# The head of a decoder layer: filler products between conditioning bursts, and an order for the first tokens written out

## The chip, the core and the metric

The kernel runs on one core of one Trainium2 chip. A core has a matrix engine (TensorE, PE in the profile; its weight loads are shown as PEld), a vector engine (VectorE, DVE), a scalar engine (ScalarE, ACT), a general engine (GpSimd, POOL) and a queue engine that issues transfers (SyncE, SP). Transfers run on 16 DMA engines that all queues share. The metric is the device time of one execution in microseconds. Before the change it was 1991.17 us, the median of three runs between 1989.67 and 1992.51.

## The reference, cut to what matters

```python
mod = jax.nn.silu(c) @ w_ada + b_ada                       # c: one row for the prompt, 8 for the samples
sh1, sc1, g1, sh2, sc2, g2 = [m[:, None, :] for m in jnp.split(mod, 6, axis=-1)]
h = _rmsnorm(x, norm1_g) * (1 + sc1) + sh1                 # x: 256 prompt tokens and 64 sample tokens, 2048 wide
p = h @ w_in                                               # 11,280 columns: q, k, v, og, u, ga, gb, alr
...                                                        # linear attention, pooling, gates, feed-forward
```

All of it is float32. This case is about the first lines only: the conditioning product `silu(c) @ w_ada` for the shift and scale of the first norm (sections 0 and 1 of six), the normed tokens `h`, and the first products of `h` with `w_in`.

## The kernel before, in words

**Layout.** The 320 tokens are kept transposed: a tile has 128 of the 2048 model columns on its partitions and the 320 tokens (T; TP = 256 prompt, TS = 64 sample) along its row, so there are 16 token tiles, KT = 16. A weight matrix is read in blocks of rows; each block lands in a buffer named raw, is copied by ScalarE to a rounded high part (whi, line 152), and VectorE takes the difference as the low part (wlo, line 153). Every product of weights with tokens is then three TensorE products (lines 166 to 168): high weights by high tokens (hh), high weights by low tokens (hl), low weights by high tokens, each 128 x 128 by 320 columns. There are three raw buffers in the main weight pool and five buffers each of whi and wlo.

**The head.** The conditioning rows c are loaded, transposed by 16 small TensorE transposes, and passed through a sigmoid to give scT. The tokens come in three tiles xn of 128, 128 and 64 rows, 2048 wide, all by SyncE's queue ahead of the first conditioning weights. A loop over the 16 token tiles makes three TensorE transposes each into a bank of `misc()` (four PSUM banks in rotation) and copies the bank to xT, on ScalarE and VectorE in turn (line 462). The sums of squares, the reciprocal root, and its broadcast rx follow (lines 473 to 486). `HeadJob` then makes the conditioning for some token tiles: `load` (line 414) issues two blocks of w_ada of 512 KB, `burst` (line 422) issues loads ahead and 32 small products in four column strips of the array (line 218), and `finish` (line 434) copies, transposes and adds the bias, so that the shift and scale (mod) stand ready. The job of the first two token tiles has four bursts over eight blocks; its blocks have eight buffers (araw). `h_unit` (line 488) then makes hh and hl of a token tile on VectorE, GpSimd and ScalarE.

**Stages.** The projection by w_in goes over five slices of token tiles, SLICES = (0,2), (2,4), (4,8), (8,12), (12,16). For each slice, a loop takes 15 units of 256 weight columns in the order q, k, v, v, u, og, og, ga, ga, gb, gb and four more gb; units of v and of the gates go by two from one block of 512 columns (`proj_pair`, line 197). After each unit, `after_unit` runs a share of a background list that prepares the next slice: the spill of xT to DRAM by GpSimd's queue, the next HeadJob's load, its four bursts and its finish, and the h_units. So in the first slice the first load comes after the second v, and the first burst (with four more loads) after u.

**What sets the order.** A scheduler orders the instructions of each engine by a simulated timeline, except those that pass through `tc.keep_in_program_order`, here also called `pinned`, which keep the order of the program among themselves. In the head all weight loads on SyncE's queue are of that kind (line 144 follows the flag in_order), and the queue is served in order: a load whose buffer is still in use holds back those behind it. For the first slice this order is, before the change: the 8 blocks of w_ada for the first job; the blocks of q, k and v; two blocks of w_ada for the second job; the block of u; four blocks of w_ada; the block of og; two blocks of w_ada; the blocks of ga and of the gbs.

Of the kernel before, what the change touches and what calls it, by code (L numbers as in the profile page):

```python
# [20 lines left out]
P = 128  # L21
TP, NB, LS = 256, 8, 8
TS = NB * LS
T = TP + TS
D = 2048
KT = D // P
# [10 lines left out]
WB = 5  # L37
AB = 3
SLICES = ((0, 2), (2, 4), (4, 8), (8, 12), (12, 16))
# [41 lines left out]
def body(tc, A):  # L81
    nc = tc.nc
    ctx = ExitStack()
    cp = ctx.enter_context(tc.tile_pool(name="cp", bufs=1))
    wp = ctx.enter_context(tc.tile_pool(name="wp", bufs=3))
# [41 lines left out]
    def tr(out, in_):  # L127
        k = in_.shape[0]
        PE.transpose(out, in_, ident[:k, :k])  # L129
# [5 lines left out]
    def raw_chunk(src, nk, nn, pool=None, tag="raw", bufs=3):  # L135

        if pool is None and more:
            more.reverse()
            if more[0] is not None:
                pool, bufs = more[0], 2  # L140
        t = (pool or wp).tile([P, nk, nn], F32, tag=tag, bufs=bufs, name=nm("raw"))
        ins = nc.sync.dma_start(t, src)
        if in_order[0]:
            tc.keep_in_program_order(ins)
        return t
# [7 lines left out]
        V.tensor_sub(lo, raw, hi.bitcast(F32))  # L153
# [16 lines left out]
    def proj(w, col, k0, k1, xh, xl):  # L170

        ps = pmain.tile([P, 2, 512], F32, tag="pm", name=nm("ps"))
        for c0 in range(k0, k1, 4):
            nk = min(4, k1 - c0)
            for j, whi, wlo in split_chunk(w[:, c0:c0 + nk, col:col + 256], nk, 256):
# [20 lines left out]

    def proj_pair(w, col, k0, k1, xh, xl):

        parts = list(split_chunk(w[:, k0:k1, col:col + 512], k1 - k0, 512))
# [171 lines left out]
    def units(h):  # L371
        return [("q", 0, OQ + DK * h), ("k", 0, OK_ + DK * h), ("v", 0, OV + DV * h),
                ("v", 1, OV + DV * h + 256), ("u", 0, OU + 256 * h),
                ("og", 0, OOG + DV * h), ("og", 1, OOG + DV * h + 256),
                ("ga", 0, OGA + DV * h), ("ga", 1, OGA + DV * h + 256),
                ("gb", 0, OGB + DV * h), ("gb", 1, OGB + DV * h + 256)]


    with tc.tile_pool(name="head", bufs=1) as xp:
# [17 lines left out]
        nc.gpsimd.dma_start(vr1[64:68, :], A["gla_norm_g"][0].rearrange("(r p) -> r p", p=P))  # L397
        pt = misc()
# [4 lines left out]
        S.activation(csig, crT, AF.Sigmoid)  # L403
        V.tensor_tensor(scT[:, :, 0:9], crT, csig, op=ALU.mult)

        def pinned(ins):
            tc.keep_in_program_order(ins)

        class HeadJob:


            def __init__(self, b0, s):
                self.b0, self.s, self.w, self.nk = b0, s, 64 * s, 8 // s
                self.ps = None
                self.raws = {}
# [19 lines left out]
            def finish(self):  # L435
                nb = self.s // 2
                sb = xp.tile([P, 2 * P], F32, tag="adasb", name=nm("adasb"))
                S.copy(sb[:, 0:self.w], self.ps[:, 0:self.w])
# [11 lines left out]


        xT = []
        for k in range(KT):
            pt = misc()
            for i in range(3):
                n = P if i < 2 else TS
                tr(pt[:, i * P:i * P + n], xn[i][:n, k * P:(k + 1) * P])
            if k < SLICES[0][1]:
                xT.append(xp.tile([P, T], F32, name="xT%d" % k))
            else:  # L460
                xT.append(hp.tile([P, T], F32, tag="hl%d" % k, name="xT%d" % k))
            (S.copy if k % 2 else V.tensor_copy)(xT[k], pt[:, 0:T])

        pt = misc()
        tr(pt[:, 0:96], vr0)
        tr(pt[:, 96:164], vr1)
# [5 lines left out]
        ssq = xp.tile([P, 3], F32, name="ssq")  # L472
        V.memset(ssq, 1.0)
        for i in range(3):
            n = P if i < 2 else TS
            S.activation(junk[:n], xn[i][:n], AF.Square, accum_out=ssq[:n, i:i + 1])
        S.activation(ssq, ssq, AF.Sqrt, scale=1.0 / D, bias=epst)
        V.reciprocal(ssq, ssq)
        prs = misc()
        dg = xp.tile([P, 3, P], F32, name="dg")  # L480
        for i in range(3):
            n = P if i < 2 else TS
            V.tensor_scalar(dg[:n, i, :n], ident[:n, :n], ssq[:n, i:i + 1], None, op0=ALU.mult)
            PE.matmul(prs[:, i * P:i * P + n], lhsT=ones[:n, :], rhs=dg[:n, i, :n], start=True, stop=True)
        rx = xp.tile([P, T], F32, name="rx")
        V.tensor_copy(rx, prs[:, 0:T])

        def h_unit(k):
            t = xp.tile([P, T], F32, tag="xh", bufs=2, name=nm("xh"))
            V.scalar_tensor_tensor(t[:, 0:TP], xT[k][:, 0:TP], modp(1, k), rx[:, 0:TP], op0=ALU.mult, op1=ALU.mult)  # L490
            G.tensor_tensor(t[:, TP:T], xT[k][:, TP:T], rx[:, TP:T], op=ALU.mult)
            G.tensor_tensor(s3(t[:, TP:T]), s3(t[:, TP:T]), mods(1, k), op=ALU.mult)
            G.tensor_tensor(s3(t[:, TP:T]), s3(t[:, TP:T]), mods(0, k), op=ALU.add)
            S.activation(hh[k][:, 0:TP], t[:, 0:TP], AF.Identity, bias=modp(0, k))
            S.copy(hh[k][:, TP:T], t[:, TP:T])
            hl[k] = hp.tile([P, T], F32R, tag="hl%d" % k, name="hl%d" % k)
            V.scalar_tensor_tensor(hl[k][:, 0:TP], t[:, 0:TP], modp(0, k), hh[k][:, 0:TP].bitcast(F32),
                                   op0=ALU.add, op1=ALU.subtract)
            V.tensor_sub(hl[k][:, TP:T], t[:, TP:T], hh[k][:, TP:T].bitcast(F32))  # L499
# [682 lines left out]
```

## Time and profile before

| | |
|---|---|
| median of three runs | 1991.17 us |
| the profiled execution | 1994.81 us, of which 1993.0 us from the first to the last instruction |
| mean granted TensorE clock | 0.991 |
| first burst of conditioning products starts | 27.1 us |
| last burst of the first job ends | 33.3 us |
| first product with w_in starts | 36.66 us |

Times inside the profile are counted from the first instruction of the profiled execution. In the rows, a line number is that of the code printed above, out<-in are the program's tile names, and xN is a count of merged instructions. The view of stretches gives each engine's busy time, the granted TensorE clock, the share of the DMA engines' time, and the rate.

### The profile page before, as it was taken

To read this page: it belongs to the slowest core of one execution; us is meant where nothing else is said; L and a number is where in the kernel's file an instruction comes from. 1 tells how busy PE (TensorE), PEld (TensorE's weight loads), DVE (VectorE), ACT (ScalarE), POOL (GpSimd) and SP (SyncE) were. 2 spreads that over 40 slices of the span, in tenths; PEclk is the share of its full clock that TensorE was granted. 3 is DMA by queue.
4 is the path that set the end of the run, shared out by engine and by line. 5 is a ranking of instruction groups with operands and counts; after the bars stand their busy time and mean duration, and the time that the engine had idled before them with its cause. 6 is when DMAs were issued, how large, how long until landed. Compare 5 with 4: busy or idle time off the path is not lost.

```text
span 1993.0 us, 37189 instructions
## 1 busy us (share of the span) xinstructions
PE 1944.7 (98%) x15014; PEld 1850.7 (93%) x15014; DVE 1014.1 (51%) x1883; ACT 819.7 (41%) x1467; POOL 138.0 (7%) x261
## 2 busy tenths in 40 slices
PE   7999999999999999999989999999999999999997
PEld 5789998898999899889989999999999999999997
DVE  2556665474546544664474444444444444444554
ACT  4333364353336433653354333343333334344443
POOL 1112220111010100110030000000000000000000
PEclk9999999999999999999989999999999999999998
DMA  8888754775975787579637666544444444444443
GB/s 290 289 298 264 231 174 144 264 267 183 326 247 162 277 274 232 169 256 323 227 113 226 202 213 200 161 155 145 150 147 153 150 152 152 150 148 147 148 138 97
DMA packets 322558, 400.83 MB, mean 201 GB/s; under 512 B 13545, under 2 KB 262633, under 8 KB 322049
## 3 DMA queue, kind: packets, MB, share of 16 engines
q1 hardware_dynamic: 310114, 358.21, 55.9%
q0 software_dynamic: 12272, 40.25, 5.4%
q8 instruction: 117, 1.92, 0.4%
q14 instruction: 55, 0.45, 0.1%
HBM read 373.96 MB, written 24.67 MB: 200 GB/s over the span
## 4 chain that ended last, share of the span: by engine, by line
PE 93%; DMA 3%; DVE 1%; ACT 1%; issue 1%; SPq 0%; POOL 0%; DVEq 0%; ACTq 0%; POOLq 0%
PE ps L166 27%; PE ps L168 27%; PE ps L167 27%; PE pm L218 5%; PE pm L129 2%; DMA raw<-w_ada 2%; PE pm L804 1%; PE pm L825 1%; DMA raw<-w_in 1%; PE pm L773 1%; DMA xn<-x_prompt 1%; DMA x<-xspill 0%; PE pm L800 0%; PE pm L762 0%; DVE wlo L153 0%
## 5 line engine op out<-in xcount | busy, mean ns | idle before, releaser
L153 DVE TENSOR_TENSOR wlo<-raw,whi 128x512 fp32r<-128x512 f32 x953 | 658.0, 695 | 819.6 <-ACT whi L152 815.1
L152 ACT CAST whi<-raw 128x512 fp32r<-128x512 f32 x953 | 586.4, 621 | 997.2 <-PE ps L167 832.4
L166 PE MATMUL ps<-hh,whi 128*128 128x320 f32 x1408 | 443.2, 315 | 6.7 <-ACT whi L152 3.3
L166 PE MATMUL ps<-h2h,whi 128*128 128x320 f32 x1408 | 437.7, 311 | 5.1 <-ACT h2h L1046 5.1
L168 PE MATMUL ps<-hh,wlo 128*128 128x320 f32 x1408 | 440.8, 313 | 0.2 <-DVE wlo L153 0.2
L167 PE MATMUL ps<-hl,whi 128*128 128x320 f32 x1408 | 438.8, 312 | 0.4 <-DVE hl L499 0.4
L168 PE MATMUL ps<-h2h,wlo 128*128 128x320 f32 x1408 | 435.7, 310 | 0.0
L167 PE MATMUL ps<-h2l,whi 128*128 128x320 f32 x1408 | 435.7, 310 | 0.0
L166 PEld LDWEIGHTS ps<-hh,whi 128*128 128x128 f32 x1408 | 265.5, 189 | 25.6 <-issue 10.2
L168 PEld LDWEIGHTS ps<-hh,wlo 128*128 128x128 f32 x1408 | 265.7, 189 | 8.6 <-issue 5.7
L166 PEld LDWEIGHTS ps<-h2h,whi 128*128 128x128 f32 x1408 | 265.2, 188 | 8.2 <-ACT h2h L1046 5.8
L167 PEld LDWEIGHTS ps<-hl,whi 128*128 128x128 f32 x1408 | 265.8, 189 | 7.5 <-issue 5.9
L167 PEld LDWEIGHTS ps<-h2l,whi 128*128 128x128 f32 x1408 | 265.2, 188 | 0.0
L168 PEld LDWEIGHTS ps<-h2h,wlo 128*128 128x128 f32 x1408 | 265.0, 188 | 0.0
L166 PE MATMUL ps<-ah,whi 128*128 128x320 f32 x704 | 218.5, 310 | 0.0
L168 PE MATMUL ps<-ah,wlo 128*128 128x320 f32 x704 | 217.7, 309 | 0.0
L167 PE MATMUL ps<-al,whi 128*128 128x320 f32 x704 | 217.6, 309 | 0.0
L167 PEld LDWEIGHTS ps<-al,whi 128*128 128x128 f32 x704 | 132.2, 188 | 0.0
L166 PEld LDWEIGHTS ps<-ah,whi 128*128 128x128 f32 x704 | 132.2, 188 | 0.0
L168 PEld LDWEIGHTS ps<-ah,wlo 128*128 128x128 f32 x704 | 132.2, 188 | 0.0
L218 PE MATMUL pm<-raw,scT 128*32 128x128 f32 (+1 forms) x2688 | 105.1, 297 | 5.9 <-DMA raw<-w_ada 5.9
L218 PEld LDWEIGHTS pm<-raw,scT 128*32 128x32 f32 x2688 | 72.3, 112 | 26.9 <-issue 13.8
(289 smaller groups left out, 1541.5 us busy)
## 6 DMA issues: line engine op xcount, KB each, us to landing
raw<-w_ada SPq DMA_DIRECT2D x192, 512.0 KB, 6.2
raw<-w_gu SPq DMA_DIRECT2D x176, 512.0 KB, 3.5
raw<-w_in SPq DMA_DIRECT2D x173, 512.0 KB, 4.4
raw<-w_down SPq DMA_DIRECT2D x79, 512.0 KB, 3.3
S<-state_gla POOLq DMA_DIRECT2D x16, 1024.0 KB, 8.3
o_gs<-S POOLq DMA_DIRECT2D x16, 1024.0 KB, 7.4
raw<-w_o SPq DMA_DIRECT2D x32, 512.0 KB, 5.0
raw<-w_down SPq DMA_DIRECT2D x15, 256.0 KB, 2.5
```

Source lines behind the costliest of these rows:

```text
L129: PE.transpose(out, in_, ident[:k, :k])
L152: S.copy(hi, raw)
L153: V.tensor_sub(lo, raw, hi.bitcast(F32))
L166: PE.matmul(ps, lhsT=whi, rhs=xhi, start=start, stop=False)
L167: PE.matmul(ps, lhsT=whi, rhs=xlo, start=False, stop=False)
L168: PE.matmul(ps, lhsT=wlo, rhs=xhi, start=False, stop=stop)
L218: ins = PE.matmul(ps[32 * j:32 * j + 32, 0:w], lhsT=scT[:, k, :], rhs=raws[j], start=k == 0 if start is None else start, stop=k == KT - 1 ...
L773: PE.matmul(pt, lhsT=E["kdn"][:, s, d * P:(d + 1) * P], rhs=E["vn"][:, s], start=s == 0, stop=s == 1)
L804: PE.matmul(pt[32 * j:32 * j + 32, :], lhsT=qeP[:, d, 4 * gg + j, :], rhs=E["S0", gg, d][:, j], start=False, stop=d == 1, tile_position=(0 ...
L825: PE.matmul(pt, lhsT=kpz[:, gg, j, d * P:(d + 1) * P], rhs=E["vp"][:, gg], start=True, stop=True)
```

## The change: what it does

The change rewrites the head, up to the first slice's loop; the loop itself and all after it are unchanged.

- **Filler.** A tile fill of 128 x 512 ones is made, and `keep_busy(n)` puts n products of 512 columns into a PSUM tile that nobody reads. There are 6 before the transposes of c, 3 after them, 10, 7 and 3 after the transposes from the three x tiles, and 4 after each of the first three bursts. All of them, the transposes of c and x, and the first strip of each conditioning product are kept in program order on TensorE.
- **Transposes.** Only the first three token tiles are transposed before the first burst; tiles 3 to 6, 7 to 11 and 12 to 15 follow the first, second and third burst. The norm's broadcast comes ahead of the third burst.
- **x_sample.** Its transfer is issued by ScalarE's queue behind the sigmoid, no longer by SyncE's queue behind x_prompt.
- **First tokens.** rx times xT is made ahead for tiles 0 and 1 (xhat), and `h_first` makes hh and hl of these tiles with all its steps in program order; tile 0's sample part goes to VectorE instead of GpSimd.
- **First weights.** The blocks of q, k, v and u are issued right after the last burst in the program; their high and low parts (`EarlySplit`) stand in program order on ScalarE and VectorE: the copy of `finish`, high of q, the steps of token tile 0, low of q, high of k, the steps of tile 1, low of k, then the rest. On SyncE's queue the block of u now stands ahead of the second job's first two blocks of w_ada.

```diff
-    def split_chunk(src, nk, nn):
+    ready = {}
+    class EarlySplit:
+        def __init__(self, raw):
...
+            self.h = wp.tile([P, 512 // n, n], F32R, tag="whi", bufs=WB, name=nm("whi"))
+            self.l = wp.tile([P, 512 // n, n], F32R, tag="wlo", bufs=WB, name=nm("wlo"))
+        def hi(self):
+            tc.keep_in_program_order(S.copy(self.h, self.raw))
+        def lo(self):
+            tc.keep_in_program_order(V.tensor_sub(self.l, self.raw, self.h.bitcast(F32)))
...
-        nc.sync.dma_start(xn[2][0:TS], A["x_sample"].rearrange("b t d -> (b t) d"))
+        idle = pmain.tile([P, 2, 512], F32, tag="pm", name=nm("idle"))
+        fill = xp.tile([P, 512], F32R, name="fill")
...
+        def keep_busy(n, tiled=0):
+            for _ in range(n):
+                tc.keep_in_program_order(PE.matmul(idle[:, 0, :], lhsT=fill[:, 0:P], rhs=fill, start=True, stop=True))
...
+        keep_busy(6)
         pt = misc()
         for k in range(KT):
-            tr(pt[:, 16 * k:16 * k + 9], crow[:, k * P:(k + 1) * P])
+            ptr(pt[:, 16 * k:16 * k + 9], crow[:, k * P:(k + 1) * P])
+        keep_busy(3)
...
+        tc.keep_in_program_order(S.activation(csig, crT, AF.Sigmoid))
+        tc.keep_in_program_order(nc.scalar.dma_start(xn[2][0:TS], A["x_sample"].rearrange("b t d -> (b t) d")))
...
+        pts = [misc() for _ in range(NX0)]
+        for i in range(3):
+            n = P if i < 2 else TS
+            for k in range(NX0):
+                ptr(pts[k][:, i * P:i * P + n], xn[i][:n, k * P:(k + 1) * P])
+            keep_busy((10, 7, 3)[i])
...
+        def h_first(k):
+            t = xhat[k]
+            E = G if k else V
+            pinned(S.activation(hh[k][:, 0:TP], t[:, 0:TP], AF.Identity, scale=modp(1, k), bias=modp(0, k)))
+            pinned(E.tensor_tensor(s3(t[:, TP:T]), s3(t[:, TP:T]), mods(1, k), op=ALU.mult))
+            pinned(E.tensor_tensor(s3(t[:, TP:T]), s3(t[:, TP:T]), mods(0, k), op=ALU.add))
+            pinned(S.copy(hh[k][:, TP:T], t[:, TP:T]))
+            hl[k] = hp.tile([P, T], F32R, tag="hl%d" % k, name="hl%d" % k)
+            pinned(V.tensor_scalar(t[:, 0:TP], t[:, 0:TP], modp(1, k), modp(0, k), op0=ALU.mult, op1=ALU.add))
+            pinned(V.tensor_sub(hl[k], t, hh[k].bitcast(F32)))
...
-        for f in HeadJob(0, SLICES[0][1]).steps():
-            f()
-        for k in range(SLICES[0][1]):
-            h_unit(k)
+        for i, k0 in enumerate(range(0, KT, 4)):
+            if i == 2:
+                x_norm()
+            job0.burst(k0)
+            while len(xT) < (7, 12, 16, 16)[i]:
+                x_trans(len(xT), len(xT) % 2)
+            if i < 3:
+                keep_busy(4)
+        ew = []
+        for kind, i, col in units(0)[:5]:
...
+            raw = raw_chunk(win[:, 0:nx, col:col + (512 if kind == "v" else 256)], nx, 512 if kind == "v" else 256)
...
+        job0.finish()
+        ew[0].hi()
+        h_first(0)
+        ew[0].lo()
+        ew[1].hi()
+        h_first(1)
+        ew[1].lo()
+        for e in ew[2:]:
+            e.hi()
+            e.lo()
```

More of the change, by code (lines that the diff above doesn't have):

```diff
@@ L154, in split, with split_chunk @@
         return hi, lo
-    def split_chunk(src, nk, nn):
+    ready = {}
+    class EarlySplit:
+        def __init__(self, raw):
+            n = raw.shape[2]
+            self.raw = raw
+            self.h = wp.tile([P, 512 // n, n], F32R, tag="whi", bufs=WB, name=nm("whi"))
[4 more added lines that the diff above has]
+            tc.keep_in_program_order(V.tensor_sub(self.l, self.raw, self.h.bitcast(F32)))
+    def split_chunk(src, nk, nn, key=None):
+        if key in ready:
+            k = 0
+            for e in ready.pop(key):
+                for j in range(e.h.shape[1]):
+                    yield k, e.h[:, j], e.l[:, j]
+                    k += 1
+            return
         raw = raw_chunk(src, nk, nn)
@@ L174, in proj @@
             nk = min(4, k1 - c0)
-            for j, whi, wlo in split_chunk(w[:, c0:c0 + nk, col:col + 256], nk, 256):
+            for j, whi, wlo in split_chunk(w[:, c0:c0 + nk, col:col + 256], nk, 256, col if w is win else None):
                 kt = c0 + j
@@ L197, in proj_pair @@
     def proj_pair(w, col, k0, k1, xh, xl):
-        parts = list(split_chunk(w[:, k0:k1, col:col + 512], k1 - k0, 512))
+        parts = list(split_chunk(w[:, k0:k1, col:col + 512], k1 - k0, 512, col))
         for half in range(2):
@@ L397, in body, with ptr @@
         nc.gpsimd.dma_start(vr1[64:68, :], A["gla_norm_g"][0].rearrange("(r p) -> r p", p=P))
+        idle = pmain.tile([P, 2, 512], F32, tag="pm", name=nm("idle"))
+        fill = xp.tile([P, 512], F32R, name="fill")
+        V.tensor_copy(fill[:, 0:P], ones)
+        for c in range(1, 4):
+            V.tensor_copy(fill[:, c * P:(c + 1) * P], ones)
+        def keep_busy(n, tiled=0):
+            for _ in range(n):
+                tc.keep_in_program_order(PE.matmul(idle[:, 0, :], lhsT=fill[:, 0:P], rhs=fill, start=True, stop=True))
+            for _ in range(tiled):
+                for j in range(4):
+                    tc.keep_in_program_order(PE.matmul(idle[32 * j:32 * j + 32, 1, :], lhsT=fill[:, 0:32], rhs=fill,
+                                                       start=True, stop=True, tile_position=(0, 32 * j)))
+        def ptr(out, in_):
+            k = in_.shape[0]
+            tc.keep_in_program_order(PE.transpose(out, in_, ident[:k, :k]))
+        keep_busy(6)
         pt = misc()
         for k in range(KT):
-            tr(pt[:, 16 * k:16 * k + 9], crow[:, k * P:(k + 1) * P])
+            ptr(pt[:, 16 * k:16 * k + 9], crow[:, k * P:(k + 1) * P])
+        keep_busy(3)
         csig = xp.tile([P, KT, 9], F32, name="csig")
         crT = pt[:, 0:256].rearrange("p (k r) -> p k r", r=16)[:, :, 0:9]
-        S.activation(csig, crT, AF.Sigmoid)
+        tc.keep_in_program_order(S.activation(csig, crT, AF.Sigmoid))
+        tc.keep_in_program_order(nc.scalar.dma_start(xn[2][0:TS], A["x_sample"].rearrange("b t d -> (b t) d")))
         V.tensor_tensor(scT[:, :, 0:9], crT, csig, op=ALU.mult)
@@ L437, in finish @@
                 sb = xp.tile([P, 2 * P], F32, tag="adasb", name=nm("adasb"))
-                S.copy(sb[:, 0:self.w], self.ps[:, 0:self.w])
+                ins = S.copy(sb[:, 0:self.w], self.ps[:, 0:self.w])
+                if self.b0 == 0:
+                    pinned(ins)
                 pt = misc()
@@ L452, in body, with x_place, x_trans @@
         xT = []
-        for k in range(KT):
+        NX0 = 3
+        def x_place(k):
+            if k < SLICES[0][1]:
+                return xp.tile([P, T], F32, name="xT%d" % k)
+            return hp.tile([P, T], F32, tag="hl%d" % k, name="xT%d" % k)
+        def x_trans(k, eng):
             pt = misc()
@@ L456, in body @@
                 n = P if i < 2 else TS
[L457 to L462, printed above, removed]
+                ptr(pt[:, i * P:i * P + n], xn[i][:n, k * P:(k + 1) * P])
+            xT.append(x_place(k))
+            (S.copy if eng else V.tensor_copy)(xT[k], pt[:, 0:T])
+        job0 = HeadJob(0, SLICES[0][1])
+        for k0 in range(0, KT, 4):
+            job0.load(k0)
+        ssq = xp.tile([P, 3], F32, name="ssq")
+        V.memset(ssq, 1.0)
+        for i in range(3):
+            n = P if i < 2 else TS
+            S.activation(junk[:n], xn[i][:n], AF.Square, accum_out=ssq[:n, i:i + 1])
+        pts = [misc() for _ in range(NX0)]
+        for i in range(3):
+            n = P if i < 2 else TS
+            for k in range(NX0):
+                ptr(pts[k][:, i * P:i * P + n], xn[i][:n, k * P:(k + 1) * P])
+            keep_busy((10, 7, 3)[i])
+        for k in range(NX0):
+            xT.append(x_place(k))
+            V.tensor_copy(xT[k], pts[k][:, 0:T])
         pt = misc()
@@ L470, in body @@
             V.tensor_scalar(bada[:, sec * KT:(sec + 1) * KT], bada[:, sec * KT:(sec + 1) * KT], 1.0, None, op0=ALU.add)
[L472 to L476, printed above, removed]
         S.activation(ssq, ssq, AF.Sqrt, scale=1.0 / D, bias=epst)
@@ L479, in body, with x_norm @@
         prs = misc()
[L480 to L484, printed above, removed]
-        rx = xp.tile([P, T], F32, name="rx")
-        V.tensor_copy(rx, prs[:, 0:T])
+        rx = xp.tile([P, T], F32, name="rx")
+        xhat = []
+        def x_norm():
+            dg = xp.tile([P, 3, P], F32, name="dg")
+            for i in range(3):
+                n = P if i < 2 else TS
+                V.tensor_scalar(dg[:n, i, :n], ident[:n, :n], ssq[:n, i:i + 1], None, op0=ALU.mult)
+                tc.keep_in_program_order(PE.matmul(prs[:, i * P:i * P + n], lhsT=ones[:n, :], rhs=dg[:n, i, :n],
+                                                   start=True, stop=True))
+            V.tensor_copy(rx, prs[:, 0:T])
+            for k in range(SLICES[0][1]):
+                t = xp.tile([P, T], F32, tag="xh", bufs=2, name=nm("xh"))
+                V.tensor_tensor(t, xT[k], rx, op=ALU.mult)
+                xhat.append(t)
+        def h_first(k):
[8 more added lines that the diff above has]
+            pinned(V.tensor_sub(hl[k], t, hh[k].bitcast(F32)))
         def h_unit(k):
@@ L528, in body @@
             early += [(ge, "gb", i, OGB + DV * h + 256 * i) for i in range(2)]
-        for f in HeadJob(0, SLICES[0][1]).steps():
-            f()
-        for k in range(SLICES[0][1]):
-            h_unit(k)
+        nx = SLICES[0][1]
+        for i, k0 in enumerate(range(0, KT, 4)):
[8 more added lines that the diff above has]
+        for kind, i, col in units(0)[:5]:
+            if kind == "v" and i == 1:
+                continue
+            raw = raw_chunk(win[:, 0:nx, col:col + (512 if kind == "v" else 256)], nx, 512 if kind == "v" else 256)
+            ready[col] = [EarlySplit(raw)] if kind != "v" else [EarlySplit(raw[:, j:j + 1]) for j in range(nx)]
+            ew += ready[col]
+        job0.finish()
[8 more added lines that the diff above has]
+            e.lo()
         for si, (k0, k1) in enumerate(SLICES):
```

## The prediction, made before the result was known

> **What bounds the kernel now.** I read the page first, then the chain of waits, then the order of time of the first 60 us, then SyncE's queue and the DMA rates of the same stretch.
>
> ```profile
> PE 93%; DMA 3%; DVE 1%; ACT 1%; issue 1%; SPq 0%; POOL 0%; DVEq 0%; ACTq 0%; POOLq 0%
> ```
>
> TensorE carries the kernel. The change touches only the head, so it is worth what it moves in the time at which TensorE gets into unbroken projection work. The chain through the kernel's first 50 us, in order of time (start, us, what):
>
> ```profile
> 1.88 10.25 DMA xn<-x_prompt
> ...
> 27.17 4.42 PE pm L218 x80
> 31.80 1.52 PE pm L218 x48
> ...
> 38.51 0.27 PE ps L168
> ...
> 41.71 0.21 PE ps L168
> ...
> 44.13 0.15 PE ps L168
> ...
> 48.24 1.01 PE pm L218 x32
> 49.32 0.38 PE ps L166
> ```
>
> The four bursts run from 27.2 to 33.3. The first 80 products cost 4.42/80 = 55 ns each and the last 48 cost 32 ns, so the clock rose at about 31.5. Projection products cost 0.27 us from 38.5 to 41.7 and 0.15 us after: a second half-speed stretch, after the pause between 33.3 and 36.66. Both are targets of the change. But the chain shows only what ended last. The start of og at 49.3, behind the second job's first burst, seems ended by TensorE; the queue shows how near another bound is. SyncE's issues (the first row merges eight loads, the second is the last of them), the spill, and ScalarE's split of og:
>
> ```profile
> 2.97 15.03 SPq L142 DMA_DIRECT2D raw<-w_ada  x8
> 16.59 1.42 SPq L142 DMA_DIRECT2D raw<-w_ada  x1
> 18.05 2.88 SPq L142 DMA_DIRECT2D raw<-w_in  x3
> 29.06 0.92 SPq L142 DMA_DIRECT2D raw<-w_ada  x2
> 33.01 0.37 SPq L142 DMA_DIRECT2D raw<-w_in  x1
> 33.47 2.07 SPq L142 DMA_DIRECT2D raw<-w_ada  x4
> 35.63 1.43 SPq L142 DMA_DIRECT2D raw<-w_in  x1
> 37.41 2.23 POOL L503 DMA_DIRECT2D xspill<-xT  x4
> 47.09 1.14 ACT L152 CAST whi<-raw 128x512 fp32r<-128x512 f32 x2 [1.64 <-DMA raw<-w_in]
> ```
>
> The block of og, issued at 35.63, ends ScalarE's wait at 47.09: landing 47.0. TensorE could have begun og about 0.7 us later, at 47.8, and begins at 49.32. The slack of the transfers there is only 1.5 us. The stretches (PE, PEld, DVE, ACT, POOL busy; clock; DMA share; GB/s):
>
> ```profile
> 9.00:11.50 2.50, 0.06 (x1) 0.00 (x0) 0.00 (x0) 1.01 (x2) 0.00 (x0) 1.00 0.98 191
> 11.50:26.00 14.50, 13.55 (x48) 7.64 (x49) 4.56 (x12) 8.72 (x15) 0.00 (x0) 1.00 1.09 352
> 26.00:30.00 4.00, 4.00 (x61) 3.44 (x64) 0.49 (x1) 1.07 (x2) 0.32 (x1) 1.00 0.05 16
> 30.00:33.50 3.50, 3.24 (x81) 2.44 (x73) 1.67 (x6) 0.17 (x2) 0.00 (x0) 1.00 0.92 295
> 34.50:47.00 12.50, 9.89 (x53) 9.37 (x54) 4.25 (x9) 4.18 (x9) 5.26 (x10) 0.86 1.01 338
> 47.00:50.50 3.50, 3.43 (x49) 3.00 (x48) 2.29 (x5) 1.73 (x3) 0.00 (x0) 1.00 1.02 374
> 50.50:64.00 13.50, 13.50 (x165) 12.32 (x164) 6.50 (x10) 7.20 (x13) 0.00 (x0) 1.00 0.67 204
> ```
>
> The DMA engines are full to 26, empty for 4 us because every buffer is taken, full again from 34.5 to 50.5, and only then have room. So the first slice up to og has two bounds 1.5 us apart: TensorE's, which the change moves, and the transfers', which restart when buffers come free.
>
> **Part 1: the bursts.** Transposes, copies of a bank, and the first and last block of w_ada with the time to landing:
>
> ```profile
> 14.26 11.03 PE L129 MATMUL pm<-cst,xn 128*128 128x128 f32 x36 [0.26 <-DVE xT L462]
> 19.84 0.43 ACT L462 COPY xT<-pm 128x320 f32<-128x320 f32 x1 [0.71 <-PE pm L129]
> 20.76 0.49 DVE L462 COPY xT<-pm 128x320 f32<-128x320 f32 x1 [0.59 <-PE pm L129]
> 1843.98 0.49 PE L129 MATMUL pm<-cst,xg 128*128 128x128 f32 x3
> 1844.23 0.39 PE L166 MATMUL ps<-ah,whi 128*128 128x320 f32 x1
> raw<-w_ada SPq DMA_DIRECT2D x1, 512.0 KB, 11.8
> raw<-w_ada SPq DMA_DIRECT2D x2, 512.0 KB, 8.9
> ```
>
> A token tile costs 11.03/12 = 0.92 us in the head, and three transposes at full speed late in the kernel take 0.25 (1843.98 to 1844.23). Between these I take 0.40, nearer the second, since two copies of 0.43 and 0.49 share few PSUM banks. A filler of 512 columns has no row; scaled from 320 columns it is 0.15 x 1.6 = 0.24 us, or 0.43 at half speed. The first block of w_ada (issued at 2.97) lands at 14.8, the last (16.59) at 25.5: eight blocks 1.53 us apart, so the first pair by 16.3, which I put at 16.0 because x_sample no longer stands ahead. Up to there the 29 fillers and nine transposes fit at full speed (behind x_prompt's last tile at 12.2: 10 fillers and 6 transposes, 2.9 us, until 15.1); at half speed they end 2 us late.
>
> From 16.0 TensorE's list is fixed: 4 bursts x 1.01 = 4.0; 13 tiles x 0.40 = 5.2; 12 fillers x 0.24 = 2.9; the norm's six small products about 0.6 (five transposes' worth at 0.25 for three, and a margin). Sum 12.7: the last burst ends at 28.7, against 33.3. Bounds: 26.5 from the last landing plus a burst; 42 with all at half speed (7.1 + 12.0 + 5.2 + 1.5).
>
> **Part 2: the first tokens.** From the rows of before:
>
> ```profile
> 32.29 1.29 DVE L153 TENSOR_TENSOR wlo<-raw,whi 128x512 fp32r<-128x512 f32 x2
> 34.31 0.18 DVE L236 TENSOR_TENSOR mod<-mod,vec 128x18 f32<-128x18 f32 x1
> 35.05 0.51 ACT L494 ACTIVATE hh<-xh,mod 128x256 fp32r<-128x256 f32 x1 [0.41 <-DVE xh L490]
> 36.36 0.24 ACT L495 CAST hh<-xh 128x64 fp32r<-128x64 f32 x1 [0.81 <-POOL xh L493]
> 36.80 0.52 DVE L497 SCALAR_TENSOR_TENSOR hl<-xh,mod,hh 128x256 fp32r<-128x256 f32 x1
> 37.87 0.21 DVE L499 TENSOR_TENSOR hl<-xh,hh 128x64 fp32r<-128x64 f32 x1
> ```
>
> mod is ready 1.2 us after the last burst (34.49 less 33.3). Then ScalarE 0.51 and 0.24: first product 2.05 us after the burst, where it was 3.35. A gain, hidden below. On VectorE, in fixed order, tile 0 takes two steps of 0.21, one between 0.21 and 0.52, one of about 0.55 that waits for ScalarE; the low part of q (0.69) is behind them and ends 3.5 us after the burst. Before, it ran from 32.29 to 32.98, ahead of the burst's end. Queued behind that step are the later VectorE steps, and, through q's raw buffer, SyncE: u is the fourth block for three raw buffers and now stands ahead of six blocks of w_ada whose own buffers have long been free.
>
> **Part 3: the transfers.** q's buffer is free at 28.7 + 3.5 = 32.2, against 33.0: 0.8 us earlier. But before, two blocks (1.05 MB) had moved in the meantime, in the stretch 30 to 33.5 (3.5 x 295 = 1.03 MB). They now come behind u and ahead of og: 1.05/0.352 = 3.0 us. og lands at 47.0 - 0.8 + 3.0 = 49.2, and is begun at 49.9, some 0.4 later in effect as its low part follows: 50.3 against 49.3.
>
> **Part 4: TensorE meanwhile.** q, k, v and u are 60 products of 0.15 = 9.0 us, with 1.3 us of waits for q's and k's late low parts and a burst of 1.0, from 2.05 after the last burst: ready for og 13.4 after it, at 42.1. It waits 8 us. Before, a pause of 3.3 us brought the half-speed stretch of 38.5 to 41.7, dearer by 0.12 us for some 12 products: 1.5 us. A pause of 8 should bring one at least; I take 1.5, between 0.8 and 2.5. The Trainium skill, "TensorE: Matmul & The Clock Gate", Part 1, says the same of idle gaps over about 3 us, so it would not alter this sum.
>
> **The sum.** +1.0 (og later) +1.5 (clock) = +2.5 us on the profiled execution's 1994.81 (span 1993.0 and 1.8 around it), so 1997.3. That execution is 3.6 above the median; on the median 1991.17 + 2.5 = 1993.7. Behind og the DMA has slack (0.67 of its time from 50.5 to 64), so nothing is made up or lost there. Moving x_sample past SyncE's loads to ScalarE's queue I cost at nothing: behind it on ScalarE wait only the squares, which need the x tiles anyway, and its bytes still pass before the last w_ada; the slow 2.5 us at 191 GB/s could give back or cost 1 us. The Trainium skill ("DMA: Bandwidth & Descriptors", Issuing engines are not separate DMA queues) says that only issue time is saved thereby; no run here shows it yet.
>
> **Rivals.** *Faster: the full queue catches up.* With seven loads issued in a row and the spill done in the pause, the rate might reach what half-microsecond stretches show:
>
> ```profile
> 42.50:43.00 0.50, 0.43 (x3) 0.30 (x3) 0.00 (x0) 0.48 (x2) 0.00 (x0) 1.00 1.15 447
> ```
>
> Data flows again about 1 us after the issue (29.06 before, and nothing until 30), so from 33.2; u, six w_ada and og, 3.93 MB, take 8.8 us at 447 GB/s, og is begun at 42.7 with hardly a pause: 49.3 - 42.7 = 6.6 us, 1984.6. Against it: the means of 338 to 374 over longer stretches. Chance 0.17.
>
> *Slower: transposes do not hold the clock.* Eleven microseconds of transposes before left the clock at half for the first 80 burst products. Between bursts there are now up to five tiles, 2.0 us at full speed, with 1 us of fillers; if one stretch of 3.4 us counts as idle, the next runs at half, where a tile costs 0.92 and lasts long enough to repeat it. In 3.4 us at half speed about half as much gets done, so each such stretch costs 1.8 us; two make the last burst 3.7 us late and og with it: +6.2, 1997.4. It decides from the point where transposes outweigh bursts and fillers in a stretch. The Trainium skill, "TensorE: Matmul & The Clock Gate", Part 4, states that transposes do not count as busy for the clock; the row of 36 agrees. Chance 0.25.
>
> *The fillers do not lift the clock at all.* The last burst ends at 42, 13 us later than forecast: 2007. Against it: plain products raised it at 31.5 within 4.4 us. Chance 0.08.
>
> **How the numbers follow.** The forecast has 0.50; its own range, from a last burst between 26.5 and 31, is 1990.5 to 1996. 0.2% is 4 us, about what a measurement of this kernel can tell from no change. Of the forecast's half 0.44 falls within that, 0.04 above and 0.02 below; of the faster rival 0.16 below, 0.01 within; of the clock rival 0.22 above, 0.03 within; the last all above. So faster 0.18, same 0.48, slower 0.34. The range goes from the faster rival, 1984.5, to 2000, past two cold stretches.
>
> **What would show it.** In the changed profile: last burst of the first job between 27 and 31; burst products at 32 ns each; q's low part some 3.5 us behind the last burst; u and six w_ada issued in one row right after it; a TensorE pause of several microseconds before og, ended by the transfer of w_in by way of ScalarE's split; half speed after it. I am wrong if og lands before 45, if TensorE runs from q into og without that pause, or if the bursts still run at 55 ns.

## The result, and the profile after

The change made the kernel slower: 2007.05 us, the median of four runs between 2004.28 and 2009.68, against 1991.76 (1989.67 to 1992.51, four runs). The ratio is 1.0079, with a 95% interval of 1.0065 to 1.0093: 13 to 19 us more. The profiled execution of the changed kernel has a span of 2006.5 us (before: 1993.0). On the chain that ended last, TensorE's share went from 93% to 90% and that of transfers from 3% to 6%.

| in the profile, us | before | forecast | after |
|---|---|---|---|
| last burst of the first job ends | 33.3 | 28.7 | 41.0 |
| first product with w_in starts | 36.66 | 30.75 | 43.03 |
| og begun | 49.32 | 50.3 | 60.11 |

Og is 10.8 us late; the first product of the third slice is 13.4 us late (125.04 against 111.63), and the span 13.5 us longer, so that most of the loss lies in the head. The chain of waits of the changed kernel, in order of time (start, us, what), tells how:

```profile
2.82 10.01 DMA raw<-w_ada
12.85 7.93 DMA xn<-x_sample
20.86 2.00 ACT junk L523 x2
...
27.02 2.00 PE idle L430 x4
29.02 1.68 PE pm L242 x32
30.70 2.86 PE pm L438 x15
33.56 1.13 PE idle L430 x4
...
39.92 1.08 PE pm L242 x32
...
44.53 4.44 DMA raw<-w_in
...
50.81 8.53 DMA raw<-w_in
...
60.11 0.41 PE ps L190
```

The chain begins with a block of w_ada (2.82), which nothing on TensorE needs yet; then comes x_sample, issued only at 12.85 and landed at 20.8. From there on the chain is TensorE's list of bursts (L242), transposes (L438) and fillers (L430), some of it at half speed: four fillers take 2.00 at 27.0 and 1.13 from 33.6 on. (The first burst is not on this stretch of it: in the built program it stands ahead of x_sample's transposes, not behind them as the program text has it, and it runs at 14.46.) Then two blocks of w_in, u's (44.53) and og's (50.81), lie on the chain one behind the other. ScalarE's rows in order of time, and one of TensorE's, show the first part from the engines' side (last bracket: idle time, and what ended it):

```profile
6.94 0.29 ACT L447 ACTIVATE csig<-pm 128x144 f32<-128x144 f32 x1 [4.92 <-PE pm L438]
12.85 0.55 ACTq L448 DMA_DIRECT2D xn<-x_sample  x1
13.59 1.91 ACT L523 ACTIVATE junk<-xn 128x2048 f32<-128x2048 f32 x1 [6.36 <-DMA raw<-w_ada]
```

```profile
20.82 0.58 PE L438 MATMUL pm<-cst,xn 64*128 64x64 f32 x3 [5.29 <-DMA xn<-x_sample]
```

The sigmoid is done at 7.2, and the transfer behind it is issued 5.6 us later. What ScalarE waited for was the landing of a block of w_ada that SyncE's queue carries. The list of waits of the built program says why: each transfer of SyncE's and ScalarE's queues signals its landing on one of eight counters, which are given out in turn over both queues, and a new use of a counter waits for the last one. x_sample was given the counter of the second block of w_ada:

```
L447 ACTIVATE csig<-pm_150 128x144 [waits PE_49]
L448 DMA xn_122<-x_sample 64x2048 [waits DMAHW5_49]
```

Then the queue of SyncE, and the one wait of it that matters (us in total, times, longest):

```profile
14.43 30.48 SPq L142 DMA_DIRECT2D raw<-w_in  x4
45.01 5.71 SPq L142 DMA_DIRECT2D raw<-w_ada  x6
50.81 1.36 SPq L142 DMA_DIRECT2D raw<-w_in  x1
```

```profile
SPq L142 <- DVE wlo L171: 26.9, 1, 26.9
```

The merged row of four loads of w_in lasts to 44.9, since u's block waits 26.9 us until q's buffer is free, which is when VectorE's low part of q ends, at 44.46. The six w_ada and og's block come behind it. The stretches show what that leaves of the transfers (columns as before: length, five engines, clock, DMA share, GB/s):

```profile
15.50:20.80 5.30, 0.04 (x4) 0.00 (x0) 0.00 (x0) 2.10 (x4) 0.00 (x0) 0.94 1.07 283
20.80:26.00 5.20, 4.67 (x15) 2.77 (x15) 2.38 (x8) 3.90 (x5) 0.00 (x0) 0.50 1.07 361
26.00:30.00 4.00, 4.00 (x28) 2.61 (x31) 0.50 (x2) 0.43 (x1) 0.00 (x0) 0.50 0.03 9
34.50:47.00 12.50, 10.62 (x101) 7.76 (x100) 7.19 (x18) 4.59 (x11) 3.20 (x7) 0.88 0.21 56
50.50:64.00 13.50, 10.21 (x85) 9.61 (x84) 2.48 (x5) 3.16 (x6) 0.00 (x0) 0.89 1.09 368
```

TensorE does nothing for 5.3 us while x_sample is awaited, then works at a clock of 0.50. The DMA engines are empty from 26 to 44.5, where before they were empty for 4 us; behind that they are full, and TensorE waits for them (10.21 busy of 13.50).

### The profile page after: what moved, and what is told of

Its sections match the earlier page's. It is cut to its first block, busy times and chain, and to the rows that moved or that the text cites. A ratio compares the mean times of both kernels' runs of the same rounds, so it can differ in the third digit from the quotient of the medians.

```text
span 2006.5 us, 37276 instructions
## 1 busy us (share of the span) xinstructions
PE 1954.6 (97%) x15055; PEld 1856.9 (93%) x15055; DVE 1017.5 (51%) x1890; ACT 818.1 (41%) x1466; POOL 134.4 (7%) x257
## 3 DMA queue, kind: packets, MB, share of 16 engines
q8 instruction: 118, 1.93, 0.4%
## 4 chain that ended last, share of the span: by engine, by line
PE 90%; DMA 6%; DVE 2%; ACT 1%; issue 1%; SPq 0%; POOL 0%; DVEq 0%; ACTq 0%; POOLq 0%
PE ps L190 26%; PE ps L192 26%; PE ps L191 26%; PE pm L242 4%; DMA raw<-w_in 3%; DMA raw<-w_ada 2%; PE pm L129 1%; DMA raw<-w_o 1%; PE pm L910 1%; PE pm L931 1%; PE pm L879 1%; DVE wlo L153 1%; ACT whi L152 0%; DMA xn<-x_sample 0%; PE pm L906 0%
## 5 line engine op out<-in xcount | busy, mean ns | idle before, releaser
L242 PE MATMUL pm<-raw,scT 128*32 128x128 f32 (+1 forms) x2688 | 103.3, 292 | 2.1 <-DMA raw<-w_ada 1.6
L242 PEld LDWEIGHTS pm<-raw,scT 128*32 128x32 f32 x2688 | 70.5, 110 | 24.1 <-issue 14.8
```

The source lines that it names most:

```text
L242: ins = PE.matmul(ps[32 * j:32 * j + 32, 0:w], lhsT=scT[:, k, :], rhs=raws[j], start=k == 0 if start is None else start, stop=k == KT - 1 ...
```

## The experiments

**The theories.** A: two waits on transfers cost the time, x_sample's late issue and u's block at the head of SyncE's queue, and the half speed is a consequence of the pauses. B, the second rival of the prediction: the transposes between the bursts lose the clock, wherever x_sample is. C: the list on TensorE has grown too long by its fillers. The runs were made on three chips, so kernels are compared by their ratios, each against the kernel before on the same chip; 0.001 is 2 us. Brackets give 95% intervals, and a difference of two ratios below about 0.002 is at the limit of the noise. Times inside a profile are those of one execution.

### x_sample's place in the changed kernel

Back on SyncE's queue, behind x_prompt (e1):

```diff
+        nc.sync.dma_start(xn[2][0:TS], A["x_sample"].rearrange("b t d -> (b t) d"))
...
-        tc.keep_in_program_order(nc.scalar.dma_start(xn[2][0:TS], A["x_sample"].rearrange("b t d -> (b t) d")))
```

> The changed kernel with one line moved back: x_sample issued by SyncE behind x_prompt. Late x_sample (theory): it lands at about 13 instead of 20.8, TensorE has no pause of 5 us and no half speed from 20.2 to 30.4, the last burst of the first job ends at 30 to 31 instead of 40.9; SyncE stays blocked by u's block until 3.5 us after that, og is begun some 19.2 us after the last burst, at 49 to 50, behind a pause with one half-speed stretch: 1993 to 1996 us. Long list (rival: fillers and fixed order on TensorE are what costs): the last burst stays at 38 or later, 2004 or more. Queue order (rival: u's block ahead of six blocks of w_ada is the main cost): little gained, 2003 or more.

Measured: 2002.09 us, 1.0053 (1.0034 to 1.0072). x_sample lands at 12.5, the first burst starts at 17.6 and the last ends at 37.7, 3.3 us earlier than in the changed kernel; but the clock is at half from 17.9 to 28.1 all the same, behind a pause of 1.93 us. There the first burst waits for the copy of a token tile, which stands on VectorE behind the norm's steps (L542 and L551), and these wait for the squares of x_sample. Theory A has the landing right and the size wrong: most of the delay in the list stayed.

The first transfer on ScalarE's queue, ahead of everything there, where all counters are free (e2: the same edit with `nc.scalar` in place of `nc.sync`):

> The changed kernel with x_sample still by ScalarE's queue, but issued as its first instruction instead of behind the sigmoid. If the late issue is what hurts (it waits at 12.85 for a block of w_ada, whose landing it shares a completion counter with): lands by 13, all as with x_sample by SyncE, 1993 to 1996. If ScalarE's queue itself is served badly next to SyncE's: landing 8 us or more after the issue still, and x_prompt or the first blocks of w_ada later than before by 1 us or more, 1997 or more. Long list: 2004 or more.

Measured: 1998.9 us, 1.0032 (1.0021 to 1.0043). x_sample is issued at 0.74 and lands at 6.9, the clock is full from 13.2 to 37.1, and the last burst ends at 33.4: with no pause and at full speed throughout, just where it ended before the change. (The list starts at 17.7, since the rows of c_sample now land later, at 6.8.) The late x_sample with what followed from it cost 1.0079 - 1.0032 = 0.0047, 9 us. B is wrong here: with the same transposes, and the fillers between them, the clock held.

The kernel before with this one edit, x_sample behind the sigmoid on ScalarE's queue (g1), measures the move by itself:

> The kernel before with one edit: x_sample's transfer behind the sigmoid on ScalarE's queue, as in the change, everything else as before. It measures that part by itself. Theory 'a transfer on another queue still waits for an earlier one': here its completion counter is shared with the first block of w_ada, so it is issued only when that block has landed, at about 14 us, and lands near 21, against 12.2 for x_prompt's last tile now; the transposes of all token tiles end later by the delay, the first burst starts at 29 to 33 instead of 27.1, and the time is 3 to 6 us longer than before, 1995 to 1998. Rival, 'x_sample was late only because ScalarE's queue was full in the change': issue at about 7.5, landing before 14, time within 1 us of before.

Measured: 2003.2 us, 1.0046 (1.0029 to 1.0064), 9 us again. ScalarE's and TensorE's rows:

```profile
10.91 0.61 ACTq L403 DMA_DIRECT2D xn<-x_sample  x1
11.70 1.91 ACT L476 ACTIVATE junk<-xn 128x2048 f32<-128x2048 f32 x1 [5.75 <-DMA raw<-w_ada]
```

```profile
18.93 0.69 PE L129 MATMUL pm<-cst,xn 64*128 64x64 f32 x4 [8.15 <-DMA xn<-x_sample]
27.75 5.55 PE L129 MATMUL pm<-cst,xn 128*128 128x128 f32 x18 [2.32 <-ACT xT L462]
```

Here the counter is that of the first block of w_ada, and the issue waits for its landing, at 10.91, when the sigmoid is done at 6.0. The bursts start at 35.6, 8.5 us late. I had expected 3 to 6 us and a first burst at 29 to 33. Part of the rest are the 2.32 us, for which TensorE waits for ScalarE, whose queue then held splits of w_in and the late copies of token tiles at once; the remainder was not followed up. Whether the place behind the sigmoid costs anything when its counter is free was not tried.

### The fillers

Without the 12 fillers between the bursts, from e2 (g2):

```diff
-            if i < 3:
-                keep_busy(4)
```

> The kernel in which x_sample is the first transfer on ScalarE's queue, without the 12 fillers between the bursts; the 29 ahead of them stay. With the 12, the clock stayed full from 13.4 to 37.3 and the last burst ended at 33.3. Theory 'the fillers between the bursts hold the clock, transposes do not': one stretch or more at half speed within the bursts, tiles at 0.92 us and a burst at 1.7 to 1.9 us there, last burst at 33 to 36 in spite of 3.4 us less work. Rival 'once lifted and with no pause, the clock holds over transposes and bursts': all bursts at 1.0 us, last burst at 29.9, and the time 1 to 3 us below that kernel's 1998.9.

Without any of the 41, from e2 (g3: the loop in `keep_busy` runs zero times):

> The same kernel without any of the 41 fillers. If fillers are what lifts and holds the clock, the transposes and at least the first two bursts run at half speed (tile 0.92 us, burst 1.7 us), the last burst ends between 33 and 38, and the time is 1998 to 2004. If plain burst products alone lift the clock within 4.4 us, as in the kernel before, the first two bursts are slow and the last two fast, last burst at 31 to 33, and the time is 1996 to 1999: the fillers would have been worth nothing.

Measured: g2 1996.64 us, 1.0017 (1.0007 to 1.0027); g3 2001.69 us, 1.0038 (1.0025 to 1.0051). TensorE's rows in the chains of g2 and of g3:

```profile
18.02 1.01 PE pm L242 x32
19.04 2.29 PE pm L439 x12
21.32 1.01 PE pm L242 x32
22.33 2.86 PE pm L439 x15
...
29.48 1.08 PE pm L242 x32
```

```profile
19.15 1.90 PE pm L439 x6
21.05 1.86 PE pm L242 x32
22.91 3.04 PE pm L439 x15
...
26.95 1.01 PE pm L242 x32
...
30.25 1.08 PE pm L242 x32
```

In g2 twelve transposes take 2.29 and a burst 1.01, all at full speed, for 12.5 us in which no filler runs; the last burst ends at 30.6 instead of 33.4. So the fillers between the bursts held nothing and were 2.9 us of list; they cost 0.0015, 3 us, which is at the limit of the noise. In g3 the products of the second burst bring the clock up by themselves (1.86, then 1.01), and the last burst ends at 31.3: all 29 fillers ahead of the bursts buy 0.8 us there. Why g3's median is 5 us above g2's, with og only 2 us later (51.83 against 49.80), stays open; its ten runs spread from 1995 to 2004.

The Trainium skill ("TensorE: Matmul & The Clock Gate", Part 4) says that transposes do not count as busy for the clock in the same way. That they lose a clock that is up, with a third of the time in burst products, g2 excludes. But they did not lift one that was down. In e1, between 17.9 and 24.7, TensorE was busy without a break for two stretches of 3.4 us, 1.95 and 1.76 us of them in transposes, and the clock stayed at half; in the next stretch, with 1.24 us of transposes, it rose at the end. In all traces six stretches of 3.4 us at half speed with more than 2.8 us of work were followed by another one at half, and in all six more than half of the work was transposes. So B is right by that much: the clock fell at a pause, and it stayed down while most of the work was transposes.

Where the clock fell here, TensorE had paused. Clock changes in all traces here lie 3.41 us apart or a multiple of it; Part 1 of that page of the Trainium skill has the same 3.4 us window, not tied to the kernel's start. In e1, and in a kernel that comes below (f1), TensorE pauses at nearly the same time, 15.7 to 17.6 and 15.1 to 17.6. Two windows of each, in step with the clock's changes, first e1, then f1:

```profile
14.44:17.85 3.41, 1.48 (x15) 1.02 (x19) 1.50 (x6) 1.73 (x4) 0.00 (x0) 1.00 1.10 347
17.85:21.27 3.42, 3.42 (x39) 2.14 (x32) 0.99 (x7) 0.43 (x1) 0.00 (x0) 0.50 1.10 349
```

```profile
12.63:16.05 3.42, 2.46 (x13) 1.77 (x12) 0.00 (x0) 3.39 (x4) 0.00 (x0) 1.00 1.10 348
16.05:19.46 3.41, 1.88 (x37) 1.35 (x37) 2.46 (x11) 0.32 (x2) 0.00 (x0) 1.00 1.10 349
```

In e1 the pause of 1.93 us falls into one window, which is left with 1.48 us of work, and the next runs at half. In f1 a pause of 2.49 us is divided between two, 2.46 and 1.88 us of work, and the clock stays. The Trainium skill puts the limit, in that page's section "Why this matters for your kernels", at pauses of about 3 us or more; here 1.93 us was enough where it fell badly. Over all windows of all traces up to the last 40 us, laid out like this, the clock fell behind every window with less than 1.45 us of work on TensorE and behind none with more than 2.05; between these, where 1.48 and 1.88 lie, it fell behind some and stayed behind others. So the work left in the window bears on it, but does not alone decide.

### u's block

Load and split back in the loop, the load behind the second job's first two blocks, in the changed kernel (e3) and in g2 (h2):

```diff
-        for kind, i, col in units(0)[:5]:
+        for kind, i, col in units(0)[:3]:
```

> The changed kernel with only the block of u put back: its load and split come from the loop, so SyncE issues two blocks of w_ada ahead of it. x_sample as changed. Late x_sample: the last burst stays at 41; two blocks (1.05 MB) move in the empty stretch, og is begun 3 us earlier, at 57: about 2004. Queue order: most of the 15 us comes back, 1995 or less. Long list: no difference, 2007.

> The same start kernel with u's block issued in the loop again, behind the second job's first two blocks, as in the kernel before. If u's place alone makes the pause ahead of og, og is begun by 46 to 47.5 and the time is 1991 to 1995. Rival: the four other w_ada blocks still stand behind u's block, and og gains only the 3 us that two blocks take at most: begun at 47 to 49, time 1994 to 1997.

Measured: e3 2003.04 us, 1.0057 (1.0040 to 1.0074), 0.0022 below the changed kernel, at the limit of the noise; h2 1989.33 us, 0.9988 (0.9980 to 0.9997), 0.0029 below g2 and below the kernel before. SyncE's queue in g2 and in h2:

```profile
16.63 17.83 SPq L142 DMA_DIRECT2D raw<-w_in  x4
34.56 5.73 SPq L142 DMA_DIRECT2D raw<-w_ada  x6
40.40 1.36 SPq L142 DMA_DIRECT2D raw<-w_in  x1
```

```profile
16.75 2.88 SPq L142 DMA_DIRECT2D raw<-w_in  x3
19.75 2.30 SPq L142 DMA_DIRECT2D raw<-w_ada  x2
33.99 0.37 SPq L142 DMA_DIRECT2D raw<-w_in  x1
34.45 2.93 SPq L142 DMA_DIRECT2D raw<-w_ada  x4
37.49 1.37 SPq L142 DMA_DIRECT2D raw<-w_in  x1
```

and TensorE's wait ahead of og, in g2 and in h2:

```profile
49.80 0.64 PE L190 MATMUL ps<-hh,whi 128*128 128x320 f32 x1 [3.41 <-ACT whi L152]
```

```profile
46.61 0.41 PE L190 MATMUL ps<-hh,whi 128*128 128x320 f32 x1 [0.58 <-ACT whi L152]
```

The last burst ends at 30.6 in g2 and at 30.5 in h2. In h2 two blocks of w_ada move in the stretch that is empty in g2, og's block is issued 2.9 us sooner, and og is begun 3.2 us sooner: the 3.0 us that the prediction gave for two blocks. A second part lies behind og: g2's pause of 3.41 is followed by half speed from 48.4 to 55.2, and the lag against the kernel before grows from 0.5 us at og to 2.9 us at the second slice (73.66 against 70.72); h2 has no half speed there.

All eight blocks of the second job ahead of u, in e1 (e4) and in g2 (h1):

```diff
+        job1 = HeadJob(SLICES[1][0], SLICES[1][1] - SLICES[1][0])
...
+            if kind == "u":
+                for j in range(4):
+                    job1.load(4 * j)
...
-                bg += HeadJob(n0, n1 - n0).steps()
+                bg += (job1 if si == 0 else HeadJob(n0, n1 - n0)).steps()
```

> x_sample by SyncE, and the second job's eight blocks of w_ada issued ahead of u's block. Late x_sample plus blocked queue: last burst at 30 to 31, the transfers run on from 26 without a pause, og lands by 41 and is begun without a pause about 13.4 us after the last burst, at 44: 5 us before the kernel before, 1985 to 1988. If the transfers were not what holds og: the same as with x_sample by SyncE alone. Long list: 2003 or more.

> The kernel with x_sample first on ScalarE's queue and no fillers between the bursts, whose last burst ended at 30.5 and og began at 49.80, with one more edit: the second job's eight blocks of w_ada issued ahead of u's block. Theory 'u's waiting block holds six loads back that og then lacks': their transfers fill the stretch from 26 to 32 that was empty, og is begun 17 us after the last burst as in the earlier kernel with that order, 47.5, and the time is 1990 to 1994, no longer than before. Rival 'the transfers of the first slices are the bound wherever they stand': og comes sooner, but TensorE waits longer between 80 and 100 for blocks of w_in (3.3 us in the kernel before), and the time stays at 1995 to 1998.

Measured: e4 1997.98 us, 1.0028 (1.0017 to 1.0039), against e1's 1.0053; h1 1996.03 us, 1.0019 (1.0009 to 1.0029), no better than g2's 1.0017. In both the transfers fill the empty stretch (h1: 364 GB/s from 26 to 30, where g2 has 6), and og no longer waits for its block. But in h1 u's block is issued at 33.81 behind the eight and takes 7.53 us instead of g2's 4.44, and TensorE waits 4.1 us:

```profile
41.37 0.62 ACT L168 CAST whi<-raw 128x512 fp32r<-128x512 f32 x1 [6.90 <-DMA raw<-w_in]
41.89 0.70 ACT L377 ACTIVATE q<-ps 128x640 f32<-128x640 f32 x1
42.64 0.63 PE L190 MATMUL ps<-hh,whi 128*128 128x320 f32 x1 [4.09 <-ACT q L377]
```

This is the first product of v, not of u. It waits until q has been copied out of one of the two PSUM tiles, and that copy stands in ScalarE's queue behind the split of u, for whose block ScalarE waits 6.90 us. (The 1.2 us ahead of v in the changed kernel, and the waits in f1 and h4 below, come about in the same way, in the last two by k's copy.) The clock is at half until 47.5, and og is begun at 51.3. The wait had moved from og to v. A version with the copies ahead of u's split was not tried. My expectation of 1985 to 1988 for e4 failed by ten: its clock was at half from 16.9 to 27.2 as in e1.

### Two versions made from the findings

f1 (x_sample on SyncE's queue, the second job's blocks ahead of u, and in `burst`'s loop fewer transposes, the rest of them in the background of the second and third slice; the transposes of `finish` in program order):

```diff
-            keep_busy((10, 7, 3)[i])
+            keep_busy((10, 7, 8)[i])
...
-            while len(xT) < (7, 12, 16, 16)[i]:
+            while len(xT) < (5, 7, 9, 9)[i]:
...
-                keep_busy(4)
+                keep_busy(3)
...
         job0.finish()
+        keep_busy(5)
...
+                bg += [lambda k=k: x_trans(k, k % 2) for k in {1: range(9, 12), 2: range(12, 16)}.get(si, ())]
```

> A version that takes the reasons found so far at their word: x_sample on SyncE's queue behind x_prompt; the second job's eight blocks of w_ada issued ahead of the block of u; only token tiles 3 to 8 transposed between the first bursts (9 to 15 in the background of the second and third slices); 10, 7 and 8 fillers behind the x tiles, 3 after each of the first three bursts, 5 after the last. If the length of TensorE's list, the late x_sample and the blocked queue were the costs: the clock full throughout, last burst at 27 to 29, og begun at 41 to 43 instead of 49.3, and 1985 to 1988. Rival, 'the clock still falls at a pause, or a wait elsewhere takes their place': og after 46 and 1992 or more.

Measured: 2000.89 us, 1.0037 (1.0022 to 1.0052). The last burst ends at 28.7, the forecast's own number; the clock is full from 5.8 to 39.9. But TensorE then waits 6.0 us ahead of v's second half, and og is begun at 49.6, as before the change. Between 130 and 140 a further 3.05 us are lost in a wait for a split of w_in, with half speed from 135.5 to 142.3. The rival won: waits elsewhere took the place of those removed.

Five fillers in TensorE's pause behind the last burst, in h1 (h4) and in h2 (k1; both keep the transposes of `finish` in program order, as f1 does, so the fillers are not the only difference):

```diff
         job0.finish()
+        keep_busy(5)
```

> As the first of this call, and five fillers in TensorE's pause behind the last burst. If that pause is what halves the clock behind it, the stretch at half speed ahead of og goes, og's readiness comes 1.5 us sooner, and the time is 0.5 to 1.5 us below the first's. Rival: og waits for its transfer, and nothing changes.

> What the runs so far point to, in one kernel: x_sample first on ScalarE's queue, no fillers between the bursts, u's block back in the loop, and five fillers in the pause behind the last burst. Without the five it began og at 46.61, took 1989.3, and had its clock halved from 34.4 to 37.8. If that stretch still cost something: no half speed after the first bursts, og begun at 45.5 to 46.3, and 1986.5 to 1988.5. Rival: og waited for its transfer by 0.6 us there, which five fillers do not bring sooner, so og stays at 46.6 and the time within 1 us of 1989.3.

Measured: h4 1993.48 us, 1.0010 (0.9999 to 1.0021), against h1's 1.0019, within the noise; k1 1991.62 us, 1.0002 (0.9994 to 1.0011), against h2's 0.9988. One stretch of h1, of h4, and TensorE's largest wait of k1 behind 40 us:

```profile
33.50:36.00 2.50, 2.46 (x10) 2.20 (x9) 2.40 (x6) 0.96 (x2) 1.33 (x3) 0.57 1.07 351
```

```profile
33.50:36.00 2.50, 2.46 (x14) 2.01 (x15) 2.40 (x5) 1.21 (x4) 1.57 (x4) 1.00 1.10 348
```

```profile
PE ps L190 <- ACT whi L152: 4.8, 3, 2.5
```

The fillers do hold the clock there (0.57 against 1.00; in h4 no half speed follows until 1010 us). But that execution of h4, 1988.05 us at a mean granted clock of 0.995, was the fastest of eleven; nine of the others had 0.990 to 0.992. In h4 og is begun at 47.7, 3.7 us sooner than in h1. In k1 TensorE comes to og sooner and waits 2.5 us for it where h2 waited 0.58; the pause is now ahead of og, which is begun at 46.18 instead of 46.61, and a half-speed stretch lies behind it, to 49.6. So k1 is as fast as the kernel before, and only h2 is a little faster, by 0.6 to 4 us; h2 is the fastest of twelve versions and was measured in one session, so that part of this may be chance.

Og's start orders the kernels nearly as their times do (f1, with its later waits, is the exception), but being earlier than before the change pays only in h2: it begins og 2.7 us sooner than before and takes 2.4 us less, while h4 begins it 1.7 sooner and k1 3.1 and gain nothing in the median. Why is not shown: these starts are those of one execution each. In k1 the half-speed stretch takes half of it back (at the second slice 1.6 us are left). Later waits for blocks of w_in are there in both h2 and the kernel before: between 60 and 140 us TensorE waits 2.6 us for splits of w_in in h2 and 3.3 before the change, with the DMA engines at 0.88 of their time or more from 80 to 100 and from 100 to 120.

## Why the prediction was wrong, point by point

- **Part 1, the bursts.** The step that failed first: "Moving x_sample past SyncE's loads to ScalarE's queue I cost at nothing". It costs 9 us, in the changed kernel (e2) and in the kernel before (g1). I asked what is queued behind the transfer, not what the transfer itself waits for. The second failure is the list: 12.7 us from the first burst's start, measured 15.7 at full speed (e2, 17.7 to 33.4). A tile costs 0.57, not 0.40; four fillers 1.13 to 1.20, not 0.96; the norm's products 0.8 to 0.9. The 0.25 behind the 0.40 ran from the start of three transposes to the start of the next product; that row itself had 0.49 for the three. So even without the late x_sample the last burst had nothing to gain on 33.3.
- **Part 2, the first tokens.** Right: the first product came 43.03 - 41.00 = 2.03 us behind the last burst, and q's low part ended 3.5 us behind it (44.46), as forecast.
- **Part 3, the transfers.** Right in mechanism: u's block held back the six, and og's block came behind them. From q's low part to og's landing I had 17.0 us (32.2 to 49.2); measured 44.5 to 59.3, 14.9. h2 measures the place of u's block, with its split, at 0.0029 of the time, 6 us, where I had put 1.0 for og being late and 1.5 for the clock.
- **Part 4, the pause.** Right in kind: TensorE waited for og, by way of ScalarE's split, with a stretch at half speed behind it. The wait was 3.3 us, not 8. About half of the difference is that og's block came sooner (18.3 us behind the last burst, not 20.5), the other that TensorE itself was slower: a wait of 1.2 ahead of v, and a half-speed stretch from 44.0 to 47.4 that I had not put behind the shorter pause of 2.03 us. From the last burst to og it was 19.1 us; I had 21.6.
- **The clock rival (1997.4).** Its sign was right, its cause half wrong: the clock fell to half for 10.2 us, in the changed kernel behind a pause of 5.3 us and in e1 behind one of 1.9, and not by transposes, which ran without losing it in e2 and g2; but once it was down, transposes did not lift it.
- **The third rival (2007).** It named the measured time, by luck: its reason does not hold, since the clock was up by 9.9 us, after fillers and transposes.
- **The faster rival.** It had no chance to show: the DMA engines moved 368 GB/s behind the pause, not 447.

By undoing one part after the other the ratio goes 1.0079, 1.0032 (x_sample early), 1.0017 (no fillers between the bursts), 0.9988 (u's block back): 9, 3 and 6 us of some 18. What is left of the change in h2, with x_sample as the first transfer on ScalarE's queue, transposes between bursts, 29 fillers ahead of them and the first tokens in fixed order, measured 0.6 to 4 us faster than the kernel before, in one session.

## What to carry to other kernels

Ask of a transfer that is moved to another queue what its own issue will wait for: buffers, and the counter on which it reports. A transfer whose buffer is not free belongs behind all those whose buffers are. And a busy loop that is to keep the clock up is worth its time only in a pause that nothing else ends later: between bursts that already hold the clock it is only more work, and ahead of a transfer that is late it only moves the pause.

## What the runs showed of the hardware that was not expected

- An issue on ScalarE's queue waited 5.6 us (changed kernel) and 5.0 us (g1) for the landing of a block that another queue carried, through a shared completion counter. The Trainium skill ("DMA: Bandwidth & Descriptors", Issuing engines are not separate DMA queues) says that moving an issue saves issue time alone; the runs add that it can cost the landing of an earlier transfer.
- A pause of 1.93 us halved the clock for 10.2 us (e1), and one of 2.49 us did not (f1).
- Transposes with a burst between them left a clock that was up at full for 12.5 us (g2), but two stretches of 3.4 us of unbroken work, 1.95 and 1.76 us of it transposes, did not lift one that was down (e1).
- Three transposes of a token tile cost 0.92 us at half speed and 0.57 at full, in a run of twelve; from a single group late in the kernel I had read 0.25.
